# Output projection of a hybrid decoder layer: six tiles by plain blocks, ten by seven half-size products

## The chip, the cores and the metric

One Trainium2 chip, one core of it. The metric is the device time of one execution in microseconds; of several executions the median is given.

## The reference, cut to what matters

One layer over 2048 tokens of width 1024, all in float32. Two mixers work side by side on one input projection: an S5 state space mixer of width 256 and a Mamba-2 (SSD) mixer of width 768. The SSD mixer ends in an RMSNorm. Their outputs are joined, multiplied by `w_out` and added to the input:

```
y = y * gelu_gate                             # S5, 256 columns
ssd = rmsnorm(y_ssd * silu(z), norm_w)        # 768 columns
x = x + concatenate([y_s5, ssd]) @ w_out      # 1024 x 1024
```

After it come a cross-attention into 256 memory tokens and a gated MLP with a causal convolution, and a final norm.

## The kernel before, in words

Tiles are 128 tokens. A float32 operand is split into a high half and a low half (`halves`, lines 95 to 102: ScalarE copies to the rounded type, VectorE subtracts), and each product of two 128-wide blocks is three matmuls (`mm3`, lines 120 to 125): high by high, high by low, low by high. A matmul takes 128 x 128 of the left operand as weights and streams 512 columns of the right.

The mixers run first. For each 512 tokens `MixerIn.ssq` (line 503) gets the sums of squares of the SSD output and makes `rs`, the factor of the RMSNorm, one number a token, kept on chip; the SSD output itself is written to `yTd` in DRAM without it (the norm's weight is in). `yTd` is laid out transposed: channels on the partitions, eight blocks of 128 channels, blocks 0 and 1 from S5 and 2 to 7 from SSD. The S5 stage (`stage_s5`, line 771) runs beside the preparation of the attention's factors `G` and `VW`. It ends with four calls of `glu` (line 868), one for each 512 tokens, which write the S5 blocks of `yTd`. They lack a factor of 0.5.

Then `stage_b` (line 1094) does the output projection, the attention scores and the attention values. In the projection the weights are all 8 x 2 blocks of `w_out`, 128 x 512 each, split and held on chip in pools Q0 to Q3 (`W`). For each of 16 tiles of tokens, `yprep` (line 1113) loads the tile of `yTd` and of `x` two tiles ahead and splits the former. For each half of the columns there are two sums on PSUM: blocks 2 to 7 (SSD) and blocks 0 and 1 (S5). VectorE adds the first, multiplied by `rs`, to the tile of `x` (line 1215), then the second, multiplied by 0.5 (line 1216). The result goes to `x1d` by POOL's DMA queue (line 1217).

The scores and the values are done by pairs of tiles in another way. `products` (line 1008) takes 256 x 1024 by 1024 x 1024 as two by two blocks and does seven products of half size instead of eight (Strassen's method in Winograd's form), in the order 1, 6, 5, 3, 7, 4, 2. Each product is 4 x 3 matmuls of 512 columns. `lefts` (line 1154) makes the seven left factors of a pair with transposes by TensorE, four sums on VectorE and seven splits; `factors` (line 1135) makes the four right factors that are sums, from four blocks, and writes them to DRAM, and `right` (line 1146) loads a right factor and splits it. `factors("G", j)` is called at tiles 2, 4, 6 and 8 of the projection, and `right("G", m)` for three of the seven m in the last three tiles and for the others behind them. `factors("VW", p)` is called in the first four pairs of the scores, `right("VW", m)` in the last pair, each m right behind the product of that number, whose buffers it takes over.

Instructions stand in the program in the order in which Python emits them. A scheduler sets the order on each engine and queue: of what its model of time says is ready and has a buffer, what was emitted first goes first. So loads on the SP queue run ahead of their place when a buffer is free; a load that waits for a buffer holds what is behind it. The pools that matter: F (10 buffers of 128 x 512, raw loads and sums), A (16, split left operands), X (6 of 128 x 1024, tiles of x), Q (7 x 8, split right operands), and 8 buffers of PSUM, which `tr4` (transposes) and the products share.

Of the kernel before, what the change touches and what calls it, by code (L numbers as in the profile page):

```python
# [9 lines left out]
F32 = mybir.dt.float32  # L10
# [3 lines left out]
ALU = mybir.AluOpType  # L14
# [15 lines left out]
class Kit:  # L30


    def __init__(self, tc, cx):
# [12 lines left out]
        nc.vector.memset(self.m05, -0.5)  # L46
        self.gains = self.cp.tile([P, 32], F32, name="gains")
# [126 lines left out]
class MixerIn:  # L174
# [328 lines left out]
    def ssq(self, b, sqacc):  # L503
        k = self.k
        for _ in range(5):
            yield
        pq = k.ps()
        for c in range(4):
            k.TE.matmul(pq[:, c:c + 1], sqacc[:, c * 128:c * 128 + 128], self.one, start=True, stop=True)
        k.rstd(self.d["rs"][:, b * 4:b * 4 + 4], pq[:, 0:4], 0.25 / 768, 1e-6)  # L510
        yield
# [259 lines left out]
def stage_s5(k, a, d, T):  # L771
# [4 lines left out]
    with ExitStack() as cx:  # L776
# [91 lines left out]
        def glu(b, gs):  # L868
            for o in range(2):
# [4 lines left out]
                V.scalar_tensor_tensor(th, th, 1.0, gf[o, b], op0=ALU.add, op1=ALU.mult)  # L874
                G.dma_start(out=d["yT"][b * 4:b * 4 + 4, :, o, :].rearrange("c p n -> p c n"), in_=th.rearrange("p (c n) -> p c n", c=4))
# [218 lines left out]
def stage_b(k, cx, a, d, T, after):  # L1094
# [5 lines left out]
    Q = lambda i: (f"Q{i}", 8)  # L1100
    xl, xp, q4, mp, ap, *qs, fp = k.pools(cx, "b", ("L", 2, 1024), ("X", 6, 1024), Q(4), ("M", 4, 576), ("A", 16), Q(0), Q(1), Q(2), Q(3), Q(5), Q(6), ("F", 10))
    qs.insert(4, q4)
    tmp = lambda: mp()[:, 0:512]
    qp = ring(8, qs)

    def split(src, pl):
        hi, lo = pl(F32R), pl(F32R)
        k.halves(src, hi, lo)
        return hi, lo

    W, ys = {}, {}
# [23 lines left out]
    def factors(nm, j):  # L1135

        r = {(q, n): k.load(d[nm][q * 4 + j][:, n * 512:n * 512 + 512], fp()) for q in range(2) for n in range(2)}
# [5 lines left out]
        for i, t in enumerate((t1, t2, t3, t4)):  # L1143
            G.dma_start(out=d[nm + "t"][i, j], in_=t)

    def right(nm, m, lo=None):
        out = []
        for j in range(4):
            src = {1: d[nm][j][:, 0:512], 3: d[nm][4 + j][:, 512:1024], 2: d[nm][4 + j][:, 0:512],
                   5: d[nm + "t"][0, j], 6: d[nm + "t"][1, j], 7: d[nm + "t"][2, j], 4: d[nm + "t"][3, j]}[m]  # L1150
            out.append(split(k.load(src, fp()), qp))
        return out

    def lefts(x0, x1):
        a11, a21, a22, a12 = (fp() for _ in range(4))
        for o, x, hf in ((a11, x0, 0), (a21, x1, 0), (a22, x1, 1), (a12, x0, 1)):
            S.activation(o, k.tr4(x, hf), AF.Copy)
        yield split(a11, ap)
# [25 lines left out]

    early = (2, 3, 6, 7)
    with k.tc.issue_after(after.ins):
        for kt in early:
            W[kt] = [split(k.load(a["w_out"][kt][:, n * 512:n * 512 + 512], fp()), qp) for n in range(2)]
    first = [yprep(t, ((256, 512), (512, 1024), (0, 256))) for t in range(2)]
    for g in first * 2:  # L1190
        next(g)
    for kt in (4, 5, 0, 1):
        W[kt] = [split(k.load(a["w_out"][kt][:, n * 512:n * 512 + 512], fp()), qp) for n in range(2)]
    for g in first * 2:
        next(g)
    head = {(t, nh): proj(ys[t][0], nh, early, last=False) for t in range(2) for nh in range(2)}
    Rg = {}
    for t in range(NT):
        if t + 2 < NT:
            list(yprep(t + 2, ((0, 512), (512, 1024))))  # L1200
        act, x = ys.pop(t)
        if t + 2 == NT:
            gen, L = xprep(0), {}
        if t + 2 >= NT:
            for _ in range(2):
                L[ORDER[len(L)]] = next(gen)
# [385 lines left out]
```

## Time and profile before

| | |
|---|---|
| median of 3 runs | 2671.1 us (2668.69 to 2675.19) |
| the profiled execution | 2667.42 us, of which the span of the trace is 2665.7 |
| mean granted clock of TensorE | 0.994 |
| TensorE busy (matmuls) | 2603.0 us, 98% |
| VectorE, ScalarE busy | 2121.5 us (80%), 1358.0 us (51%) |
| POOL busy | 407.3 us (15%) |
| DMA | 480.94 MB, 180 GB/s over the span |

The engines are TensorE (PE, its weight loads PEld), VectorE (DVE), ScalarE (ACT) and GpSimd (POOL); SP issues most of the loads. An instruction's line is that of the helper that issued it, so a matmul of any stage is at lines 123 to 125, and its operands tell the stage: Q and A are the right and left operands of stage B. Busy time is a share of time and says nothing of how closely instructions of one engine follow one another; for that the starts in the timeline are read.

### The profile page before, as it was taken

Reading aid. Unit: us, or ns where it says so; the run is one execution under the profiler, and the core shown is the slowest. Engines: PE = TensorE matmul, PEld = TensorE weight load, DVE = VectorE, ACT = ScalarE, POOL = GpSimd, SP = SyncE. Lnnn points to the kernel's source line nnn. Section 1 sums busy time; section 2 is a strip of 40 time slices with the busy share of each in tenths; the row PEclk is TensorE's granted clock in tenths of the full one; section 3 lists DMA queues with packets and bytes.
Section 4 is the critical chain, followed back from the end, with each engine's and each line's share of the span. In section 5 each row is a group of like instructions: output and inputs, shape, how many; then the busy total and the mean of one; then the engine's idle time right before and its main releaser. Section 6 shows DMA issues by size and latency. Waiting matters only on the chain. (4 is left out here: it accounts for less than half of the span.)

```text
span 2665.7 us, 38967 instructions
## 1 busy us (share of the span) xinstructions
PE 2603.0 (98%) x12796; PEld 2150.3 (81%) x12796; DVE 2121.5 (80%) x4034; ACT 1358.0 (51%) x2817; POOL 407.3 (15%) x691
## 2 busy tenths in 40 slices
PE   8999999999999999999999999999999999999998
PEld 6768878788987888888888888888888887788876
DVE  8798898888876537778788878989787877678776
ACT  4655567764556116788554545445444434433333
POOL 1112212111022101202202332212111110000000
PEclk9999999999999999999999999999999999999999
DMA  5565554543586936546762444344222218887886
GB/s 188 173 186 175 182 192 164 164 139 126 177 303 235 336 126 213 182 168 231 261 202 83 128 146 133 103 123 153 80 87 80 87 64 280 278 283 249 262 263 209
DMA packets 244355, 480.94 MB, mean 180 GB/s; under 512 B 30584, under 2 KB 72824, under 8 KB 244152
## 3 DMA queue, kind: packets, MB, share of 16 engines
q1 hardware_dynamic: 182312, 341.38, 38.3%
q0 software_dynamic: 32976, 118.09, 13.8%
q10 hardware_dynamic: 28864, 18.98, 2.3%
q8 instruction: 101, 1.65, 0.3%
q14 instruction: 102, 0.84, 0.1%
HBM read 363.25 MB, written 114.49 MB: 179 GB/s over the span
## 5 line engine op out<-in xcount | busy, mean ns | idle before, releaser
L124 PE MATMUL ps<-H,W 128*128 128x512 f32 x952 | 370.6, 389 | 0.3 <-DVE H L99 0.3
L123 PE MATMUL ps<-H,W 128*128 128x512 f32 x952 | 370.8, 390 | 0.0
L125 PE MATMUL ps<-H,W 128*128 128x512 f32 x952 | 370.4, 389 | 0.0
L123 PE MATMUL ps<-h,w 128*128 128x512 f32 (+1 forms) x736 | 299.1, 406 | 3.1 <-DVE h L102 2.1
L124 PE MATMUL ps<-h,w 128*128 128x512 f32 (+1 forms) x736 | 286.6, 389 | 0.9 <-DVE h L102 0.9
L125 PE MATMUL ps<-h,w 128*128 128x512 f32 (+1 forms) x736 | 286.3, 389 | 0.7 <-DVE w L99 0.7
L123 PE MATMUL ps<-Q,A 128*128 128x512 f32 x704 | 275.8, 392 | 0.8 <-ACT A L98 0.8
L125 PE MATMUL ps<-Q,A 128*128 128x512 f32 x704 | 274.5, 390 | 0.2 <-DVE A L99 0.2
L124 PE MATMUL ps<-Q,A 128*128 128x512 f32 x704 | 273.9, 389 | 0.0
L98 ACT ACTIVATE W<-S 128x512 fp32r<-128x512 f32 x191 | 119.0, 630 | 292.8 <-DVE S L1346 146.1
L98 ACT ACTIVATE w<-r 128x512 fp32r<-128x512 f32 x224 | 139.4, 627 | 139.5 <-PE ps L124 108.7
L124 PEld LDWEIGHTS ps<-H,W 128*128 128x128 f32 x952 | 178.7, 188 | 38.0 <-DVE H L99 1.1
L125 PEld LDWEIGHTS ps<-H,W 128*128 128x128 f32 x952 | 178.7, 188 | 37.2
L123 PEld LDWEIGHTS ps<-H,W 128*128 128x128 f32 x952 | 178.7, 188 | 37.0 <-ACT H L98 0.3
L99 DVE TENSOR_TENSOR w<-r,w 128x512 fp32r<-128x512 f32 x224 | 153.5, 687 | 33.0 <-ACT w L98 31.4
L125 PEld LDWEIGHTS ps<-h,w 128*128 128x128 f32 x736 | 139.4, 189 | 30.6 <-DVE w L99 1.1
L123 PEld LDWEIGHTS ps<-h,w 128*128 128x128 f32 x736 | 139.6, 190 | 29.7 <-DVE h L102 2.3
L124 PEld LDWEIGHTS ps<-h,w 128*128 128x128 f32 x736 | 139.8, 190 | 27.6 <-DVE h L102 2.5
L125 PEld LDWEIGHTS ps<-Q,A 128*128 128x128 f32 x704 | 132.2, 188 | 29.1 <-DVE A L99 1.4
L123 PEld LDWEIGHTS ps<-Q,A 128*128 128x128 f32 x704 | 132.2, 188 | 27.8 <-ACT A L98 1.0
L124 PEld LDWEIGHTS ps<-Q,A 128*128 128x128 f32 x704 | 132.3, 188 | 26.6
L98 ACT ACTIVATE A<-F 128x512 fp32r<-128x512 f32 (+1 forms) x146 | 89.1, 631 | 126.4 <-PE ps L124 74.1
(474 smaller groups left out, 6187.4 us busy)
## 6 DMA issues: line engine op xcount, KB each, us to landing
A<-actd SPq DMA_DIRECT2D x192, 256.0 KB, 3.6
r<-in_w_in SPq DMA_DIRECT2D x176, 256.0 KB, 2.9
R<-in_w_up SPq DMA_DIRECT2D x176, 256.0 KB, 2.8
R<-in_w_down SPq DMA_DIRECT2D x132, 256.0 KB, 4.3
actd<-U POOLq DMA_DIRECT2D x88, 256.0 KB, 3.1
A<-actd SPq DMA_DIRECT2D x96, 192.0 KB, 3.6
R<-h3Cd SPq DMA_DIRECT2D x56, 256.0 KB, 3.2
L<-acsd POOLq DMA_DIRECT2D x32, 384.0 KB, 4.4
```

The lines of the kernel that those rows point to most:

```text
L98: self.S.activation(hi, src, AF.Copy)
L99: self.V.tensor_tensor(lo, src, hi.bitcast(F32), op=ALU.subtract)
L123: self.TE.matmul(out, lh, rh, start=first and i == 0, stop=False)
L124: self.TE.matmul(out, lh, rl, start=False, stop=False)
L125: self.TE.matmul(out, ll, rh, start=False, stop=last and i == n - 1)
```

## The change

The SSD norm's factor is taken out of the sum: the S5 blocks are divided by it, so that one sum over all eight blocks can be multiplied by `rs`. `ssq` makes `iv` = 0.5 / `rs` as well (a power on POOL) and writes it to DRAM; `glu` loads it, broadcast to all partitions, and multiplies with it.

The first three pairs of tiles (six tiles) are done by plain blocks as before, now with one sum per half and one scaled addition. Beside tiles 1 to 4, four blocks of `w_out` are loaded again for each j, and `tfour` makes the four sums from them; three of them are split on chip for right factors 6, 5 and 7, the fourth goes to `Otd` in DRAM and is loaded and split for right factor 4 behind the sixth tile, into the buffers of the plain weights that are no longer needed. Right factors 1, 2 and 3 are blocks of the plain weights already there. The other five pairs are done by `products`. Their left factors come from `yTd` without transposes (`ypair`). `factors("G")` moves to the first four of these pairs, and all seven `right("G", m)` to the last one. The pools of right operands are named by m and by half (`at`), at the same places of memory in sum.

```diff
         pq = k.ps()
         for c in range(4):
             k.TE.matmul(pq[:, c:c + 1], sqacc[:, c * 128:c * 128 + 128], self.one, start=True, stop=True)
+        iv = self.sp.tile([P, 4], F32, tag="iv", name="iv")
+        k.V.tensor_scalar(iv, pq[:, 0:4], 0.0625 / 768, 0.25e-6, op0=ALU.mult, op1=ALU.add)
         k.rstd(self.d["rs"][:, b * 4:b * 4 + 4], pq[:, 0:4], 0.25 / 768, 1e-6)
+        k.G.tensor_tensor(iv, iv, k.p05[:, 0:1].to_broadcast([P, 4]), op=ALU.pow)
+        k.G.dma_start(out=self.d["iv"][b].rearrange("(c p) -> p c", p=P), in_=iv)
         yield
...
         def glu(b, gs):
+            iv = k.t()
+            G.dma_start(out=iv, in_=d["iv"][b].partition_broadcast(P))
             for o in range(2):
...
                 V.scalar_tensor_tensor(th, th, 1.0, gf[o, b], op0=ALU.add, op1=ALU.mult)
+                V.tensor_tensor(th, th, iv, op=ALU.mult)
...
+    at = lambda m, j: qs[f"Q{m}{'ba'[j // 2]}"]
+    PLAIN = 3
...
+    kt_at = {(0, 0): 1, (0, 1): 4, (1, 0): 2, (1, 1): 3}
+
+    def wload(kt):
+        W[kt] = [split(k.load(a["w_out"][kt][:, n * 512:n * 512 + 512], fp()), at(kt_at[kt // 4, n], kt % 4)) for n in range(2)]
...
-        if t + 1 == NT:
-            for kts in ((2, 3), (6, 7)):
-                for nh in range(2):
-                    head[t, nh] = proj(act, nh, kts, head.get((t, nh)), last=False)
-        for nh in range(2):
-            s = slice(nh * 512, nh * 512 + 512)
-            p2 = proj(act, nh, (4, 5), head[t, nh]) if (t, nh) in head else proj(act, nh, range(2, 8))
-            p1 = proj(act, nh, [0, 1])
-            V.scalar_tensor_tensor(x[:, s], p2, d["rs"][:, t:t + 1], x[:, s], op0=ALU.mult, op1=ALU.add)
-            V.scalar_tensor_tensor(x[:, s], p1, 0.5, x[:, s], op0=ALU.mult, op1=ALU.add)
-        G.dma_start(out=d["x1"][t * 128:t * 128 + 128, :], in_=x)
-        if t in (2, 4, 6, 8):
-            factors("G", t // 2 - 1)
-        if t >= NT - 3:
-            Rg[ORDER[t - NT + 3]] = right("G", ORDER[t - NT + 3])
...
+    def ypair(p):
+        rows = []
+        for t in (2 * p, 2 * p + 1):
+            rows.append(k.load(d["yT"][t].rearrange("p a b -> p (a b)"), xp()))
+        (a11, a12), (a21, a22) = ((y[:, 0:512], y[:, 512:1024]) for y in rows)
+        return parts(a11, a21, a22, a12)
+    Rw, Rg, L = {5: [], 6: [], 7: []}, {}, {}
+    for t in range(2 * PLAIN):
+        j = t - 1
+        r = blocks(a["w_out"], j) if 0 <= j < 4 else None
+        if t + 2 < 2 * PLAIN:
+            list(yprep(t + 2, ((0, 512), (512, 1024))))
+        act, x = ys.pop(t)
+        if t == 2 * PLAIN - 3:
+            gen = ypair(PLAIN)
+        if t >= 2 * PLAIN - 2:
+            for _ in range(2):
+                L[ORDER[len(L)]] = next(gen)
+        for nh in range(2):
+            s = slice(nh * 512, nh * 512 + 512)
+            p = proj(act, nh, (4, 5, 0, 1), head[t, nh]) if (t, nh) in head else proj(act, nh, range(8))
+            V.scalar_tensor_tensor(x[:, s], p, d["rs"][:, t:t + 1], x[:, s], op0=ALU.mult, op1=ALU.add)
+        G.dma_start(out=d["x1"][t * 128:t * 128 + 128, :], in_=x)
+        if r:
+            t1, t2, t3, t4 = tfour(r)
+            G.dma_start(out=d["Ot"][j], in_=t4)
+            for m, v in ((6, t2), (5, t1), (7, t3)):
+                Rw[m].append(split(v, at(m, j)))
+    for m, q, n in ((1, 0, 0), (2, 1, 0), (3, 1, 1)):
+        Rw[m] = [W[q * 4 + j][n] for j in range(4)]
+    ahead = ypair(PLAIN + 1)
+    for m in ORDER[4:]:
+        L[m] = next(gen)
+    Rw[4] = [split(k.load(d["Ot"][j], fp()), at(4, j)) for j in range(4)]
+    for p in range(PLAIN, NP):
+        xs = []
+        for t in (2 * p, 2 * p + 1):
+            xs.append(xp())
+            nc.sync.dma_start(out=xs[-1], in_=a["x"][t * 128:t * 128 + 128, :])
+        gen, ahead = ahead, ypair(p + 2) if p + 2 < NP else xprep(p + 2 - NP)
+
+        def put(i, j, x, y, op):
+            c = tmp() if (i, j) == (1, 1) else x if i else y
+            V.tensor_tensor(c, x, y, op=op)
+            x = xs[i][:, j * 512:j * 512 + 512]
+            V.scalar_tensor_tensor(x, c, d["rs"][:, 2 * p + i:2 * p + i + 1], x, op0=ALU.mult, op1=ALU.add)
+
+        def after(m):
+            L[m] = next(gen)
+            if p + 1 == NP:
+                Rg[m] = right("G", m)
+            if m == 3 and p < PLAIN + 4:
+                factors("G", p - PLAIN)
+        products(k, terms(L, Rw), tmp, put, after)
+        for i in range(2):
+            t = 2 * p + i
+            G.dma_start(out=d["x1"][t * 128:t * 128 + 128, :], in_=xs[i])
...
-    ahead = xprep(1)
-    for m in ORDER[1:]:
-        if m not in Rg:
-            Rg[m] = right("G", m)
-        if m not in L:
-            L[m] = next(gen)
```

## Rows read from the trace of the kernel before

**Rows 1.** The page: busy time by engine; the granted clock in 40 slices.

```profile
PE 2603.0 (98%) x12796; PEld 2150.3 (81%) x12796; DVE 2121.5 (80%) x4034; ACT 1358.0 (51%) x2817; POOL 407.3 (15%) x691
...
PEclk9999999999999999999999999999999999999999
```

**Rows 2.** Busy time in stretches: us, then PE, PEld, DVE, ACT, POOL, clock, DMA share, GB/s.

```profile
836.00:848.00 12.00, 11.21 (x44) 8.41 (x45) 9.88 (x17) 11.61 (x24) 1.53 (x2) 0.86 0.59 193
...
870.00:890.00 20.00, 20.00 (x90) 16.57 (x89) 9.85 (x16) 3.71 (x6) 3.28 (x6) 1.00 1.00 363
...
970.00:990.00 20.00, 20.00 (x90) 16.57 (x89) 7.64 (x12) 1.90 (x3) 1.06 (x2) 1.00 0.13 52
...
1240.00:1260.00 20.00, 20.00 (x106) 17.05 (x105) 15.47 (x29) 14.78 (x39) 7.47 (x11) 1.00 0.71 239
```

**Rows 3.** The costliest groups: the first matmuls of stage B's products.

```profile
L123 PE MATMUL ps<-Q,A 128*128 128x512 f32 x704 | 275.8, 392 | 0.8 <-ACT A L98 0.8
```

**Rows 4.** Timeline of the projection, PE: start, duration; 39 matmuls between the two.

```profile
899.91 0.39 PE L123 MATMUL ps<-Q,A 128*128 128x512 f32 x1
...
908.75 0.39 PE L123 MATMUL ps<-Q,A 128*128 128x512 f32 x1
```

**Rows 5.** Timeline of the end of the scores, DVE.

```profile
1195.17 2.49 DVE L99 TENSOR_TENSOR Q<-F,Q 128x512 fp32r<-128x512 f32 x4
1197.58 0.69 DVE L1265 TENSOR_TENSOR X<-ps,M 128x512 f32<-128x512 f32 x1
```

**Rows 6.** Groups of DVE, 848 to 1031 us: busy, mean ns, idle before.

```profile
L1139 DVE TENSOR_TENSOR F<-F 128x512 f32<-128x512 f32 x4 | 2.8, 690 | 11.0 <-DMA F<-Gd 11.0
L1140 DVE TENSOR_TENSOR F<-F 128x512 f32<-128x512 f32 x4 | 2.8, 690 | 4.4 <-DMA F<-Gd 4.4
```

**Rows 7.** Timeline of the scores, PE: transposes of two successive pairs.

```profile
1154.40 1.91 PE L148 MATMUL ps<-ident,L 128*128 128x128 f32 x16
...
1175.22 1.91 PE L148 MATMUL ps<-ident,L 128*128 128x128 f32 x16
```

**Rows 8.** Waits of PE, 1000 to 1400 us: total, times, longest.

```profile
PE ps L123 <- ACT A L98: 0.8, 1, 0.8
PE ps L1068 <- ACT F L1157: 0.4, 1, 0.4
PE ps L124 <- DVE H L99: 0.3, 1, 0.3
```

**Rows 9.** Timeline of POOL: the sixth of sixteen writes of a finished tile.

```profile
926.36 0.54 POOL L1217 DMA_DIRECT2D x1d<-X  x1 [2.78 <-DVE X L1216]
```

**Rows 10.** Timeline of the SP queue: reads of G, first and fourth round.

```profile
866.24 2.37 SPq L111 DMA_DIRECT2D F<-Gd  x4
...
909.48 0.91 SPq L111 DMA_DIRECT2D F<-Gd  x2
...
913.18 2.56 SPq L111 DMA_DIRECT2D F<-Gd  x2
```

**Rows 11.** DMA issues: count, KB each, median us to landing.

```profile
L<-acsd POOLq DMA_DIRECT2D x32, 384.0 KB, 4.4
...
F<-in_w_out SPq DMA_DIRECT2D x16, 256.0 KB, 5.1
Gtd<-F POOLq DMA_DIRECT2D x16, 256.0 KB, 4.4
F<-Gtd SPq DMA_DIRECT2D x16, 256.0 KB, 4.5
```

**Rows 12.** Timeline of the end of the S5 stage and the first tiles, PE and DVE.

```profile
836.79 0.73 PE L123 MATMUL ps<-t 128*128 128x512 f32 x2 [1.94 <-ACT t L98]
...
853.97 4.29 DVE L99 TENSOR_TENSOR Q<-F,Q 128x512 fp32r<-128x512 f32 x7
858.47 0.69 DVE L99 TENSOR_TENSOR Q<-F,Q 128x512 fp32r<-128x512 f32 x1 [0.21 <-ACT Q L98]
...
864.96 0.75 DVE L1215 SCALAR_TENSOR_TENSOR X<-ps,rs,X 128x512 f32<-128x512 f32 x1
```

More of the change, by code (lines that the diff above doesn't have):

```diff
@@ L46, in __init__ @@
         nc.vector.memset(self.m05, -0.5)
+        self.p05 = self.cp.tile([P, 1], F32, name="p05")
+        nc.vector.memset(self.p05, 0.5)
         self.gains = self.cp.tile([P, 32], F32, name="gains")
@@ L1098, in stage_b @@
     NP = NT // 2
-    Q = lambda i: (f"Q{i}", 8)
-    xl, xp, q4, mp, ap, *qs, fp = k.pools(cx, "b", ("L", 2, 1024), ("X", 6, 1024), Q(4), ("M", 4, 576), ("A", 16), Q(0), Q(1), Q(2), Q(3), Q(5), Q(6), ("F", 10))
-    qs.insert(4, q4)
+    q5 = [("Q5b", 4), ("Q5a", 4)]
+    late = [(f"Q{m}b", 4) for m in (1, 4, 3, 2)]
+    first = [(f"Q{m}a", 4) for m in (1, 4, 3, 2)]
+    names = [n for n, _ in q5 + first + late] + [f"Q{m}{h}" for m in (6, 7) for h in "ba"]
+    xl, xp, q50, q51, mp, ap, *qs, fp = k.pools(cx, "b", ("L", 2, 1024), ("X", 6, 1024), *q5, ("M", 4, 576), ("A", 16), *first, *late, *((n, 4) for n in names[10:]), ("F", 10))
+    qs = dict(zip(names, [q50, q51] + qs))
     tmp = lambda: mp()[:, 0:512]
-    qp = ring(8, qs)
+    at = lambda m, j: qs[f"Q{m}{'ba'[j // 2]}"]
+    PLAIN = 3
     def split(src, pl):
@@ L1133, in proj, with blocks, tfour @@
         return p
-    def factors(nm, j):
-        r = {(q, n): k.load(d[nm][q * 4 + j][:, n * 512:n * 512 + 512], fp()) for q in range(2) for n in range(2)}
+    def blocks(src, j):
+        return {(q, n): k.load(src[q * 4 + j][:, n * 512:n * 512 + 512], fp()) for q in range(2) for n in range(2)}
+    def tfour(r):
         t1, t2, t3, t4 = fp(), fp(), r[0, 1], r[1, 0]
@@ L1142, in factors @@
         V.tensor_tensor(t4, t2, r[1, 0], op=ALU.subtract)
-        for i, t in enumerate((t1, t2, t3, t4)):
+        return t1, t2, t3, t4
+    def factors(nm, j):
+        for i, t in enumerate(tfour(blocks(d[nm], j))):
             G.dma_start(out=d[nm + "t"][i, j], in_=t)
@@ L1150, in right @@
                    5: d[nm + "t"][0, j], 6: d[nm + "t"][1, j], 7: d[nm + "t"][2, j], 4: d[nm + "t"][3, j]}[m]
-            out.append(split(k.load(src, fp()), qp))
+            out.append(split(k.load(src, fp()), at(m, j)))
         return out
@@ L1157, in lefts, with parts @@
             S.activation(o, k.tr4(x, hf), AF.Copy)
+        yield from parts(a11, a21, a22, a12)
+    def parts(a11, a21, a22, a12):
         yield split(a11, ap)
@@ L1227, in terms @@
         return f
+    early = (2, 3, 6, 7)
+    with k.tc.issue_after(after.ins):
+        for kt in early:
+            wload(kt)
+    begin = [yprep(t, ((256, 512), (512, 1024), (0, 256))) for t in range(2)]
+    for g in begin * 2:
+        next(g)
+    for kt in (4, 5, 0, 1):
+        wload(kt)
+    for g in begin * 2:
+        next(g)
+    head = {(t, nh): proj(ys[t][0], nh, early, last=False) for t in range(2) for nh in range(2)}
+    def ypair(p):
[4 more added lines that the diff above has]
+        return parts(a11, a21, a22, a12)
```

24 lines of the change are left out of this document (1 added, 23 removed).

## Prediction, made before the changed kernel was run

> **What bounds the kernel now.** I read the page first, then the stretch of the projection, then the two places outside it that resemble what the change puts there. The page: TensorE (PE) is busy 98% of the span at a granted clock of 9 or more tenths in every slice [rows 1]. In the projection it has no gap at all: 20.00 of 20 us at 870 and at 970 us, at full clock, while VectorE (DVE) works 9.85 and 7.64 us [rows 2]. So here a matmul taken off PE is time taken off the end, as long as nothing else becomes late. How much time: the duration of one matmul in the groups, 389 to 392 ns [rows 3], is a latency; matmuls overlap. The pace is the step between starts. From the start at 899.91 to that at 908.75 us there are 39 matmuls of 128x512: 8.84 / 39 = 0.2267 us each [rows 4]. The group of line 123 with 704 matmuls [rows 3] is the whole of stage B: 256 of the projection (16 tiles x 2 halves x 8 blocks), 224 of the scores and 224 of the values (8 pairs x 7 products x 4 each); lines 124 and 125 hold as many again.
>
> **What the products give.** Before: 256 x 3 = 768 matmuls. After: six plain tiles, 6 x 2 x 8 x 3 = 288, and five pairs, 5 x 7 x 4 x 3 = 420; 708 in all, 60 fewer. yT lies in memory with its contraction on the partitions, so the new left factors need no transposes; those of x1 stay as they are. 60 x 0.2267 = **13.6 us** less. The two projection sums of a half (blocks 2 to 7, blocks 0 and 1) become one, with the same matmuls. The Trainium skill states another price: its page "TensorE: Matmul & The Clock Gate", section "Back-to-back issue gap", gives some 131 ns for a 512-column matmul in a sustained stream. By it the 60 would be worth 7.9 us as an estimate, and the gain after the losses below under the 0.3% line. The trace's 0.2267 us is the same kind of stream in this kernel, so it decides, and no chance goes to the other.
>
> **VectorE and ScalarE in the five pairs.** A DVE instruction of 128x512 takes a step of 0.602 us where it is not waiting: four in 2.41 us, 1195.17 to 1197.58 [rows 5]. A pair needs 7 low halves and 4 sums for the left factors, 11 for the products (two sums on PSUM for U2 and U4, one for U3, and two instructions for each of four quadrants), and, in pairs 3 to 6, 4 for `factors("G")`: 26 x 0.602 = 15.7 us against 84 x 0.2267 = 19.0 us of PE. The values stage has this very load, and there PE is busy 20.00 of 20 us beside 15.47 of DVE [rows 2]. I cost it at nothing; the cover is the 3.3 us that DVE has left per pair. `factors("G")` comes with four reads on SP and four writes on POOL. Where it stood, DVE waited 11.0 and 4.4 us for those reads, in all four calls [rows 6]; 3.9 us a call would use up the cover, and the low halves of the next pair's left factors are queued behind. But the reads stood there beside the reload of weights and a DVE with nothing else to do; in the pairs they are issued at the fourth product, with three products more before the next pair, so I take no loss, and 0.6 us a pair as the other bound. In the plain tiles a reload of four `w_out` blocks adds 4 sums and 3 splits, 7 x 0.602 = 4.2 us, and two scaled additions instead of four take 1.2 away; per 10.9 us tile (48 x 0.2267) DVE then has some 11 instructions, 6.6 us. Nothing lost there either.
>
> **The last pair.** `right("G")` makes 28 low halves; they stood beside the last three plain tiles, and now stand in pair 7. DVE has 50 x 0.602 = 30.1 us there, PE 19.0 and 1.8 for 16 transposes (a scores pair with its transposes takes 1175.22 - 1154.40 = 20.82 us [rows 7]). It falls 9.3 us behind. The nearest row is the end of the scores, where the same code makes the 28 factors of VW beside the same left factors, 7 sums and the softmax: 46 such instructions and more. The waits of PE there come to 0.8 + 0.4 + 0.3 us [rows 8], for eight PSUM buffers and factors made ahead take up the rest. Bounds 0 and 9.3; I take 1.4, since the row is the same code.
>
> **The switch from plain to seven products.** PE needs the right factors for product 6 one product (2.7 us) after the switch, those of product 4, which go out to Ot and come back, five products (13.6 us) after. In the old trace the sixth tile leaves at 926.4 [rows 9], so PE switches at about 925. The reload is the twin of the old reads of G: four blocks, four subtractions. Four such rounds were issued, the first at 866.2 and the last at 909.5 us [rows 10], so 14.4 us apart on the mean, one every second tile in the program. The new ones stand one tile earlier and every tile. Even at the old rhythm the last lands at 909.5 + 3.7 (its second half was issued at 913.2) + 5.1 for `w_out` [rows 11] = 918.3, and with 7 instructions is split by 922.5; Ot is written (4.4) and read (4.5) [rows 11] and split (4 x 0.602) by 934, needed at 925 + 13.6 = 938.6. Cost nothing, with 5 us to spare. Queued on SP behind these loads are yT and x of the next tiles. The x of pair 3 waits on SP for the writes of tiles 4 and 5, but is first needed at the fourth product, 10.9 us after the switch.
>
> **The end of the S5 stage.** Eight DVE multiplications, 8 x 0.602 = 4.8 us, four broadcasts on POOL's queue (nearest: the broadcast of acs, 4.4 us to landing [rows 11]) and four small tiles. All four `glu` calls lie at 836 to 854 us. From 853.97 DVE makes seven low halves of `w_out` in 4.29 us without a gap, and the last at 858.47 [rows 12]; the scaled additions of `glu` stand before them. The first projection sum is read at 864.96 [rows 12]. So 4.8 us more on DVE meets some 4 to 5 us of cover: a loss of 0 to 1 us. If a broadcast is late, DVE waits with all those low halves behind it, and PE after them. PE already waits 1.94 us at 836.79 [rows 12], and the clock of that stretch is 0.86 [rows 2], so 28% of 12 us at the lower of its two levels, which costs another 1.7. Moving tiles in that pool can save this or double it: bounds -3 and +4; I take +0.7, near the plain count. The square roots for `iv` (a power on POOL and one small write in each of four blocks) lie beside work that PE does not wait for.
>
> **Sum.** -13.6 + 1.4 + 0.7 = -11.5 us. The profiled execution took 2667.4 us (span 2665.7), 3.7 under the median of 2671.1; applied to the median, **2659.6 us**, 0.43% less. About 0.3% (8 us) is what a measurement of this kernel can tell from no change.
>
> **Rivals.**
> *DVE is late in the last pair for its whole arithmetic.* 9.3 us come back: -13.6 + 9.3 + 0.7 = -3.6, 2667.5. For it: 30.1 against 20.8. Against it: the 1.5 us of the scores' end [rows 8].
> *DMA, not PE, sets the pace of the first tiles.* The share of the DMA engines is 1.00 at 870 to 890 us with 363 GB/s [rows 2]; were matmuls merely spread by their data, taking some away gains nothing, and the reload only replaces reads of G: 2671. Against it: matmuls come as densely where the share is 0.13, with 90 in 20 us at both places [rows 2]. The Trainium skill warns of the busy share of matmuls, in "Perfetto Trace Analysis", section "Identifying the Most-Contended Engine": weight loads are to be looked at. The rows agree that weights load for 16.57 of 20 us, so the share alone proves little; the equal counts are what I rest on.
> *Right factors late at the switch (slower).* If a round of four reloads is spaced by more than (927.7 - 9.3 - 866.2) / 3 = 17.4 us, PE stands still at product 6; the 9.3 are landing and splitting. Spaced by 21 it eats the gain. At 24, because SP holds `w_out` loads behind an x or a yT load that waits for a buffer, PE loses 3 x 6.6 = 19.8 and some 2 more at the lower clock: -11.5 + 21.8 = +10.3, 2681. For it: four rounds now stand in four tiles, on the queue that carries everything. Against: 14.4 us between rounds in the old trace, with writes of Gt beside them that are gone.
> That the matmuls aren't fewer can't be: the loops are unrolled and their counts fixed.
>
> **Chances.** The forecast 0.62; an S5 end that shifts in our favour, near 2656, 0.05; DVE late 0.14; DMA pace 0.06; the switch a few us late, near 2667, 0.04; the switch late enough to be slower 0.09. So faster 0.67, within 0.3% 0.24, slower 0.09. The low end is the full 13.6 with 3 us from the S5 end, 2654.5; the high end takes in the DVE rival and the spread of the runs, 2669. Left out are the slower case and most of the DMA one, some 0.15.
>
> **What would show it.** Right: 684 matmuls in each of the three groups of Q and A; steps of 0.2267 us; pairs of projection 19.1 us apart with PE full; the scores starting some 12 us earlier; DVE full and PE waits under 2 us at the last pair; rounds of `w_out` reads under 17 us apart. Wrong: waits of PE on low halves or on PSUM at the switch or before the scores, a drop of the granted clock there, or a longer gap before the first projection matmul with DVE waiting for `iv`.

## The result, and the profile after

The changed kernel takes 2684.8 us (median of 5; 2681.7 to 2695.5) against 2671.1 for the kernel before beside it: ratio 1.0062, interval 1.0047 to 1.0078, 0.6% slower. Forecast were 2659.6 and a range of 2654.5 to 2669.0; the sign is wrong. The executions of one kernel spread by up to 14 us (one of e5, at 6689 us, is left out), so below a stage is read from one profile and a whole from ratios.

The matmuls went as counted. In the page after, PE has 60 instructions fewer than in [rows 1], and its idle share has grown.

```profile
PE 2598.9 (97%) x12736; PEld 2142.8 (80%) x12736; DVE 2167.0 (81%) x4117; ACT 1379.5 (51%) x2853; POOL 421.4 (16%) x707
...
PEclk9999999999999999999999999999999999999999
```

Three stretches lost this again, and more. Busy time by stretches after (columns as in [rows 2]): the entry of S5, the first tiles, a pair of the projection, its last pair, the first pair of the scores.

```profile
732.00:736.00 4.00, 4.00 (x36) 4.00 (x35) 1.25 (x3) 0.63 (x1) 1.51 (x3) 1.00 1.28 147
736.00:740.00 4.00, 2.09 (x18) 1.89 (x16) 0.00 (x0) 0.48 (x1) 0.00 (x0) 1.00 0.78 134
740.00:744.00 4.00, 2.28 (x9) 1.99 (x10) 3.77 (x7) 2.77 (x7) 0.00 (x0) 0.70 0.98 362
...
870.00:890.00 20.00, 16.61 (x72) 13.42 (x73) 14.75 (x25) 5.15 (x9) 3.55 (x5) 1.00 0.89 311
...
970.00:990.00 20.00, 20.00 (x90) 16.58 (x89) 16.30 (x30) 4.75 (x8) 4.84 (x8) 1.00 0.64 215
...
1008.05:1028.85 20.80, 20.80 (x101) 17.48 (x100) 17.46 (x32) 10.38 (x23) 2.18 (x4) 1.00 0.70 244
1028.85:1058.87 30.02, 23.33 (x101) 18.39 (x100) 27.90 (x50) 21.72 (x42) 2.59 (x4) 0.94 0.84 288
```

*Entry of S5.* Between 732 and 740 us the DMA engines are busy at 1.28 and 0.78 (a share over 1 means packets that overlap) and move 147 and 134 GB/s. From 734 us DVE has no work and ACT 0.48 us of it, then PE has none, and the granted clock falls to 0.70 of full, a mean over its two levels, 1.2 and 2.4 GHz. Before, the same 732 to 736 us read so:

```profile
732.00:736.00 4.00, 4.00 (x33) 3.73 (x32) 1.95 (x4) 2.55 (x6) 0.00 (x0) 1.00 1.03 399
```

What POOL issued just ahead is the last of four writes of `iv`, 512 numbers of 4 bytes each; this is the view of `ivd` after, with the writes and the four later copies.

```profile
L516 POOL DMA_DIRECT2D ivd<-iv x4: 799/808/811, 266.9 to 727.9; - x4
L876 POOL DMA_DIRECT2D t<-ivd x4: 538/554/554, 843.4 to 863.8; - x4
...
  DVE t L883: 3.8, 2
```

The view of `iv` has the four writes alone; 2 KB take 8 to 12 us to land:

```profile
DMA to landing us min/median/max: 8.3/9.6/11.7
```

*End of S5.* DVE waits 3.59 us for a broadcast of `iv`, behind it stand the low halves that PE needs (timelines of DVE and PE after). That answers to [rows 12], where DVE had no such gap. From the first projection matmul to the end of the sixth tile it takes 71.8 us, 67.7 before.

```profile
869.83 2.50 DVE L883 TENSOR_TENSOR t<-t 128x512 f32<-128x512 f32 x4 [3.59 <-DMA t<-ivd]
```

```profile
872.98 0.50 PE L127 MATMUL ps<-Q2a,A 128*128 128x512 f32 x1 [3.15 <-DVE A L101]
```

*Behind the last pair.* In the last pair itself (the stretch from 1008.05 us) PE is full. The first pair of the scores takes 30.0 us, 20.8 before. These are the first matmuls of the first two pairs of the scores, in the timeline after:

```profile
1028.85 0.39 PE L125 MATMUL ps<-Q1b,A 128*128 128x512 f32 x1
...
1058.87 0.39 PE L125 MATMUL ps<-Q1b,A 128*128 128x512 f32 x1
```

DVE is busy 27.90 of these 30.02 us, with low halves of G's right factors and the last evacuations of the projection (line 1271, in `put`), and PE waits for the latter. The waits of PE from 1000 to 1400 us, against the 1.5 us of [rows 8]:

```profile
PE ps L125 <- DVE M L1271: 6.5, 3, 2.7
PE ps L125 <- DVE su L1297: 1.4, 1, 1.4
PE ps L125 <- ACT H L100: 0.9, 1, 0.9
```

Between them, from 880 to 1020 us, PE is full, the pairs and the switch included.

### The profile page after: what moved, and what is told of

Read it like the earlier page. It is cut to its first block, busy times and chain, and to the rows that moved or that the text cites. A ratio compares the mean times of both kernels' runs of the same rounds, so it can differ in the third digit from the quotient of the medians.

```text
span 2680.0 us, 39005 instructions
## 1 busy us (share of the span) xinstructions
PE 2598.9 (97%) x12736; PEld 2142.8 (80%) x12736; DVE 2167.0 (81%) x4117; ACT 1379.5 (51%) x2853; POOL 421.4 (16%) x707
## 3 DMA queue, kind: packets, MB, share of 16 engines
q1 hardware_dynamic: 183752, 346.62, 39.9%
## 5 line engine op out<-in xcount | busy, mean ns | idle before, releaser
L315 DVE SCALAR_TENSOR_TENSOR t<-t,cw 128x512 f32<-128x512 f32 x168 | 129.0, 768 | 13.9 <-ACT t L313 12.9
L101 DVE TENSOR_TENSOR W<-S,W 128x512 fp32r<-128x512 f32 x191 | 130.5, 686 | 7.9 <-ACT W L100 6.2
L100 ACT ACTIVATE W<-R 128x512 fp32r<-128x512 f32 x124 | 76.6, 628 | 112.9 <-PE ps L126 102.3
L1464 DVE SCALAR_TENSOR_TENSOR U<-G,C,U 128x512 f32<-128x512 f32 x176 | 122.9, 748 | 13.5 <-POOL G L1457 8.7
L127 PE MATMUL ps<-W,B 128*128 128x512 f32 x308 | 121.8, 396 | 6.9 <-DVE B L101 6.1
L1513 DVE TENSOR_TENSOR A<-A 128x512 f32<-128x512 f32 (+1 forms) x120 | 77.0, 645 | 60.7 <-DMA A<-actd 59.5
```

Of the source, the lines that this page charges most:

```text
L100: self.S.activation(hi, src, AF.Copy)
L101: self.V.tensor_tensor(lo, src, hi.bitcast(F32), op=ALU.subtract)
L127: self.TE.matmul(out, ll, rh, start=False, stop=last and i == n - 1)
L315: k.V.scalar_tensor_tensor(xc, gb[:, q:q + 512], cw[:, j, q:q + 1], xc, op0=ALU.mult, op1=ALU.add)
L1464: V.scalar_tensor_tensor(q4(c), g[:, :, q:q + 128], cw[:, i, q:q + 1], q4(c), op0=ALU.mult, op1=ALU.add)
L1513: V.tensor_tensor(raws[0], raws[0], raws[1], op=op(l[2]))
```

## The experiments

All comparisons are with the kernel before, run beside each. "Rows" below is the kernel of e5. The columns are: the stretch from the first load of `in_wqT` to the first of `in_wo` (SP queue); the start of the first projection matmul; from it to the first matmul of the seventh tile (not given where the order of the tiles is another); the first two pairs of the scores; the time from the first projection matmul to the last transposes of the values; ratio and interval.

| kernel | wqT to wo | projection starts | six tiles | two scores pairs | to the values' end | ratio |
|---|---|---|---|---|---|---|
| before | 24.3 | 848.6 | 67.7 | 41.6 | 484.3 | 1 |
| after | 29.4 | 860.1 | 71.8 | 50.8 | 484.4 | 1.0062 (1.0047 to 1.0078) |
| e1 no iv | 23.7 | 849.1 | 67.7 | 52.6 | 484.1 | 0.9992 (0.9981 to 1.0003) |
| e2 iv alone | 30.2 | 865.1 | 72.4 | 41.6 | 489.3 | 1.0038 (1.0024 to 1.0051) |
| e3 iv on chip | 23.5 | 876.2 | 65.3 | 51.1 | 478.3 | 1.0069 (1.0051 to 1.0087) |
| e4 priority | 30.2 | 862.9 | 72.2 | 52.5 | 486.1 | 1.0064 (1.0041 to 1.0087) |
| e5 rows | 21.2 | 849.7 | 68.6 | 50.7 | 481.4 | 1.0000 (0.9989 to 1.0011) |
| e8 early copies | 31.7 | 861.5 | 69.7 | 49.8 | 481.7 | 1.0062 (1.0047 to 1.0077) |
| e6 rows, no low halves | 21.6 | 848.8 | 68.9 | 50.2 | 481.7 | 0.9999 (0.9990 to 1.0009) |
| e7 rows, GpSimd | 21.6 | 851.3 | 69.2 | 57.5 | 488.7 | 1.0041 (1.0026 to 1.0056) |
| e9 rows, 7 reads | 21.7 | 848.7 | 68.7 | 47.2 | 478.2 | 0.9988 (0.9979 to 0.9998) |
| e10 rows, neither | 21.8 | 854.5 | 70.2 | 45.8 | 477.2 | 0.9976 (0.9965 to 0.9987) |
| e13 rows, no factors | 21.8 | 853.4 | 72.3 | 41.6 | 475.8 | 0.9976 (0.9965 to 0.9988) |
| e15 no iv, no factors | 24.6 | 852.9 | 67.7 | 41.6 | 470.4 | 0.9965 (0.9953 to 0.9978) |
| e11 plain pair last | 21.9 | 853.5 | - | 41.6 | 489.9 | 1.0025 (1.0014 to 1.0036) |
| e12 and early sums | 22.1 | 852.6 | - | 41.6 | 482.8 | 0.9994 (0.9983 to 1.0006) |
| e14 and lighter | 22.3 | 855.0 | - | 41.6 | 477.3 | 0.9996 (0.9986 to 1.0005) |
| e16 and early scale | 21.9 | 851.5 | - | 41.6 | 481.3 | 0.9992 (0.9981 to 1.0004) |

### The inverse root: e1 to e3, e5, e8

**e1**, the changed kernel without `iv`.

```diff
-        k.G.dma_start(out=self.d["iv"][b].rearrange("(c p) -> p c", p=P), in_=iv)
...
-                V.tensor_tensor(th, th, iv, op=ALU.mult)
```

> The changed kernel without iv: neither the square root and the write in ssq nor the broadcast and the multiplications in glu (the S5 blocks of yT lack their factor). Theory 1, from the two traces: what iv brings (the writes of 4 bytes an element at the entry of the S5 stage, POOL's queue in the mixer, the broadcasts at its end) costs 10 to 14 us, so this runs at 2668 to 2675 us, and the S5 stage's first matmul of line 834 is back near 755 us. Rival: the losses come from the order in which the scheduler puts things since the program differs, and iv itself is cheap: 2680 to 2688 us. If only the last pair had cost anything, it would also stay above 2680.

2669.8 us, ratio 0.9992. The loss goes, but none of the 13.6 us shows as a gain.

**e2**, the kernel before with `iv` and one factor for both sums.

```diff
-            V.scalar_tensor_tensor(x[:, s], p1, 0.5, x[:, s], op0=ALU.mult, op1=ALU.add)
+            V.scalar_tensor_tensor(x[:, s], p1, d["rs"][:, t:t + 1], x[:, s], op0=ALU.mult, op1=ALU.add)
```

> The kernel before with iv alone: ssq, glu and the factor rs in place of 0.5 on the second sum; the projection stays sixteen plain tiles. Theory 1: slower than before by 10 to 14 us, 2681 to 2685, nearly all of it ahead of the first projection matmul; the projection itself as long as before. Rival: iv lies beside other work, 2669 to 2674 us, and the loss of the changed kernel is in the pairs.

Ratio 1.0038, 10 us more, without any of the products. So `iv` by itself costs most of it.

**e3**, `iv` kept on chip and spread by four diagonal matrices and four matmuls by ones in each `glu`.

```diff
+            for c in range(4):
+                cs = slice(c * 128, c * 128 + 128)
+                V.tensor_scalar(dg[:, cs], k.ident, d["iv"][:, b * 4 + c:b * 4 + c + 1], None, op0=ALU.mult)
+                TE.matmul(iv[:, cs], ones, dg[:, cs], start=True, stop=True)
```

> The changed kernel with iv kept on chip: one small tile for all tokens, and in glu four diagonal tiles and four matmuls by ones that spread it over the partitions, with no DMA. Theory 1 (the DMAs of iv are what costs): 2668 to 2676 us, some 1 us above the run without iv. Rival (the multiplications on VectorE and the power on POOL are what costs, or the scheduler's order): 2680 us and more.

A miss: ratio 1.0069. The entry of S5 is back at 23.5 us, but PE, in order, now waits in `glu` for the diagonals behind a busy DVE (waits of PE, 720 to 900 us):

```profile
PE ps L880 <- DVE t L879: 17.1, 4, 6.4
```

**e5**, the same factor in another form: collected on chip in a 128 x 16 tile, turned once, written as 16 rows of 512 bytes, the copies read at the start of S5.

```diff
+        TE.transpose(pv[0:T // 128, 0:P], d["iv"][:, :], k.ident)
+        S.activation(ivr, pv[0:T // 128, 0:P], AF.Copy)
+        G.dma_start(out=d["ivd"], in_=ivr)
```

> Edit: the changed kernel, with the inverse roots kept in a small tile on chip; at the start of S5 four PE instructions' worth of work turn the 128x16 tile round once, one DMA writes it as 16 rows of 512 bytes, and the four copies for all partitions are read right after, into tiles of their own. The 16 multiplications in the gated units stay. Theory 1 (the 4-byte writes and the late copies cost the time, the multiplications do not): 2671, between 2667 and 2676; from the first in_wqT load to the first in_wo load about 24 us, no wait of DVE on the copies in the gated units. Rival (the scheduler's other order and the added VectorE work cost it, however the factor travels): 2680 or more.

2669.7 us, ratio 1.0000: the loss of the change is gone with all its arithmetic still there (the multiplications are 8, not 16). The entry of S5 takes 21.2 us.

**e8**, the 4-byte writes kept, only the copies early.

```diff
-            iv = k.t()
-            G.dma_start(out=iv, in_=d["iv"][b].partition_broadcast(P))
...
+        for b in range(T // 512):
+            G.dma_start(out=ivs[b], in_=d["iv"][b].partition_broadcast(P))
         inp(0)
```

> Edit: the changed kernel with its four writes of 512 x 4 bytes as they are, but the four copies for all partitions read early in S5 into tiles of their own, instead of one ahead of each gated unit. Theory 1 with two shares (the writes cost some 5 us at the entry of S5, the late copies some 4 us at its end): 2681, between 2678 and 2684, that is 7 to 12 us more than the kernel with rows; the stretch from the first in_wqT load to the first in_wo load stays near 29 us. Rival (the writes cost nothing that PE waits for, all of it is the late copies): within 3 us of the kernel with rows.

2684.5 us, just above my range: the late copies cost nothing in the sum, and more than the 5 us of my share hangs on the writes, since e5 differs from this kernel in their form alone. S5 in this kernel stops in full for 4 us while the last of them lands (same columns as above):

```profile
736.00:740.00 4.00, 3.59 (x31) 3.39 (x29) 0.69 (x1) 0.63 (x1) 0.00 (x0) 1.00 1.18 204
740.00:744.00 4.00, 0.00 (x0) 0.00 (x0) 0.00 (x0) 0.00 (x0) 0.00 (x0) 0.93 0.75 195
```

Early copies take 2.1 us off the six tiles and put 2.3 on the entry, so the wait for a broadcast seen in the kernel after is not what the change lost by. In the table every kernel with 4-byte writes has 29 to 32 us in the first column, every other 21 to 25.

### The last pair: e4, e6, e7, e9, e10, e13, e15

**e4**, the changed kernel, evacuations of the last projection pair put ahead of the splits.

```diff
+        with k.tc.high_priority(pri) if pri else nullcontext():
...
-        products(k, terms(L, Rw), tmp, put, after)
+        products(k, terms(L, Rw), tmp, put, after, 200 if p + 1 == NP else 0)
```

> The changed kernel with a higher priority for what reads the products of the last projection pair (the copy and the sums on PSUM and the scaled additions), so that they go ahead of the splits of G's right factors on VectorE. Theory 2: PE's 6.5 us of waits there and some 2 us at the lower clock are waits for PSUM behind those splits; 5 to 8.6 us come back, 2676 to 2680 us. Rival: VectorE's load of 30 us in that pair is what counts, whatever its order; PE then waits for G's right factors in the first pair of the scores instead, and the time stays at 2682 to 2687.

A miss: ratio 1.0064. The waits on line 1271 went; PE then waited in the first pair of the scores for the right factors and at the second for a left one, and the two take 52.5 us against 50.8. Order moved the wait, not the sum.

**e6**, rows without the 28 low halves.

```diff
+                hi = at(m, j)(F32R)
+                S.activation(hi, src, AF.Copy)
+                out.append((hi, hi))
```

> Edit: the kernel of the run before (rows) with one more: the 28 right factors of the scores that are made in the last projection pair have no low halves (the products use the high half twice, so the matmul count stays; the low part of G is left out of the computation). Theory 2 (VectorE's load in the last pair costs some 8 us): 8 us less than the kernel with rows, between 5 and 10, and PE busy over 19.5 of every 20 us from 1000 to 1060. Rival (the reads of the factors, or ScalarE, would take VectorE's place): at most 3 us less.

A miss: ratio 0.9999. I had held VectorE alone for the cause. With e5 and e6 side by side (stretches, columns as above) DVE falls from 18.91 to 6.00 us, and PE still does 69 matmuls where 98 fit; the DMA engines are at 0.93 and 0.88. The two scores pairs take 50.2 us, 50.7 in e5.

```profile
1020.00:1040.00 20.00, 14.38 (x54) 10.53 (x55) 18.91 (x33) 15.67 (x31) 1.11 (x2) 0.91 0.93 321
```

```profile
1020.00:1040.00 20.00, 15.96 (x69) 12.31 (x67) 6.00 (x13) 14.53 (x29) 1.45 (x3) 1.00 0.88 338
1040.00:1060.00 20.00, 18.79 (x79) 15.77 (x80) 16.68 (x32) 15.30 (x36) 3.51 (x7) 0.83 0.53 172
```

PE's wait is now one of 4.4 us on ScalarE's copy of a left factor of the second scores pair, whose rows of x1 were issued on SP behind the last reads of G (waits of PE, 1000 to 1060 us).

```profile
PE ps L125 <- ACT A L100: 4.4, 1, 4.4
```

**e7**, rows with half of the low halves on GpSimd.

```diff
+                G.tensor_tensor(lo, src, hi.bitcast(F32), op=ALU.subtract)
```

> Edit: the kernel with rows, and 14 of the 28 low halves of the scores' right factors in the last projection pair are subtracted by GpSimd instead of VectorE. Theory 2: VectorE is relieved of 14 x 0.60 = 8.4 us of its some 60 in 1000 to 1066, so the 8 us of PE waits shrink by at least half: 4 to 8 us less than the kernel with rows, below the kernel before. Rival (GpSimd is slower at it than 1.5 us each, or holds VectorE up): the same as the kernel with rows or slower, and PE waits on the low halves that GpSimd makes.

The rival held: ratio 1.0041. GpSimd takes some 1.3 us for one and stops VectorE meanwhile (last section).

**e9**, rows with 7 reads instead of 28, and **e10**, with 7 reads and no low halves (the edits of e9 and e6 together).

```diff
+            if j == 0:
+                one = k.load(src, fp())
+            out.append(split(one, at(m, j)))
```

> Edit: the kernel with rows; of the scores' 28 right-factor blocks made in the last projection pair only 7 are read (each of the seven factors takes its first block four times; the other three blocks of each are left out of the computation), all 28 are still split in two halves. Theory 3 (in the last pair VectorE and the reads are both full, and either alone keeps PE waiting some 10 us): the same as the kernel with rows, within 3 us, with PE still waiting on VectorE. Rival (the reads alone set the pace, VectorE is late only beside them): 6 to 10 us less.

> Edit: the kernel with rows, with 7 reads instead of 28 and no low halves for the scores' right factors (both left out of the computation; the matmul count stays). Theory 3: 8 to 12 us less than the kernel with rows, about 2660, and PE busy over 19.5 of every 20 us from 1000 to 1060. Rival (something else, such as ScalarE's copies or the second pair of x1 rows, holds PE there): within 3 us of the kernel with rows.

Ratios 0.9988 and 0.9976. Low halves away gives 0.0%, reads away 0.1%, both away 0.24%; with intervals of 0.1% either way that doesn't show whether both give more than the sum of the two. And 0.24% is 6.4 us and not the 8 to 12 expected. The two scores pairs say more: of the 9.1 us that they lose in e5, the low halves give back 0.5, the reads 3.6, both 4.9. Without the reads DVE is the full one (26.30 of 26.30 us in the first scores pair of e9), and without both ScalarE (19.11 of 20 us in e10, where PE waits for it). These are the stretches of e9 and e10, columns as above, and PE's wait in e10 from 1020 to 1050 us:

```profile
1014.50:1040.80 26.30, 22.61 (x102) 18.55 (x100) 26.30 (x48) 18.03 (x38) 2.69 (x4) 0.94 0.42 141
```

```profile
1020.00:1040.00 20.00, 17.80 (x84) 14.51 (x83) 11.13 (x22) 19.11 (x41) 2.22 (x4) 0.95 0.56 195
```

```profile
PE ps L125 <- ACT M L1033: 2.2, 1, 2.2
```

So three limits lie close together, and relieving one leaves the next. A rival was not tried: the factors start late. In e5 DVE is busy 11.34 us of the last projection pair's 20.80 and 28.52 of the next 29.90, and ScalarE, in order, stands 6.0 us for the rows of x1 before its first copy of a factor (stretches and ScalarE's timeline of e5).

```profile
994.40:1015.20 20.80, 20.80 (x101) 17.47 (x100) 11.34 (x22) 9.60 (x21) 2.18 (x4) 1.00 0.50 177
1015.20:1045.10 29.90, 23.70 (x101) 18.16 (x100) 28.52 (x51) 22.57 (x43) 2.60 (x4) 0.94 0.90 299
```

```profile
1003.92 0.63 ACT L1059 ACTIVATE F<-L 128x512 f32<-128x512 f32 x1 [5.99 <-DMA L<-x1d]
```

**e13**, rows with no right factors made in the last pair at all.

```diff
-                Rg[m] = right("G", m)
+                Rg[m] = Rw[m]
```

> Edit: the kernel with rows, with the last projection pair making none of the scores' right factors (no reads, no copies, no low halves: the scores use the projection's factors in their place, so G is left out of the computation; the matmul count stays). Theory 4 (all of the missing gain of 13.6 lies in making the right factors inside the one last pair; ScalarE's 28 copies are the part that the kernel with neither reads nor low halves still paid): 10 to 14 us less than the kernel with rows, about 2658, and under 1 us of PE waits from 1000 to 1060. Rival (part of the gain is lost in another place, such as the end of S5 or the switch): the same as with neither reads nor low halves, about 2664.

In the profile the pairs are healed, 98 matmuls in 20 us throughout and 41.6 us for the two scores pairs. The whole came to 2661.7 against 2668.3, less than expected and the rival's number. To the values' end 8.5 us of the 13.6 are there; 4.6 are lost at the end of S5, at 860 us, where the six tiles take 72.3 us against 67.7 (stretches of e13).

```profile
860.00:880.00 20.00, 17.58 (x70) 13.72 (x69) 12.77 (x22) 4.97 (x9) 2.43 (x4) 0.91 0.95 340
1020.00:1040.00 20.00, 20.00 (x98) 16.82 (x97) 14.80 (x28) 9.30 (x20) 2.21 (x4) 1.00 0.47 159
```

**e15**, neither right factors nor `iv` (the edits of e13 and e1).

> Edit: the changed kernel without the inverse roots (as in the first experiment) and with the last projection pair making none of the scores' right factors (S5's factor and G are left out of the computation). Account: of the 13.6 us that 60 matmuls are worth, the last pair took some 10 and the multiplications at the end of S5 some 3. With both gone nothing is left to take: 2656 against about 2670 before, between 2653 and 2660, and PE full from 840 to 1100 as in the kernel before. Rival (there is a third loss in the projection, or the matmuls are worth less than their pitch): 2662 or more.

Both places are full (stretches of e15):

```profile
860.00:880.00 20.00, 20.00 (x90) 16.54 (x89) 11.49 (x20) 5.98 (x12) 2.67 (x5) 1.00 0.95 330
1020.00:1040.00 20.00, 20.00 (x98) 16.78 (x98) 11.24 (x22) 7.96 (x18) 2.21 (x4) 1.00 0.49 159
```

From the first projection matmul to the values' end it takes 470.4 us, 13.9 less than before, where 60 matmuls are worth 13.6. The whole is 2662.3 against 2672.2, ratio 0.9965: 9.4 us, not 14, and the rival's number, though the stretch leaves no room for its reasons. In its profile, the slowest of its six executions, S5 ended 4 us later and the stages after the values took some 10 longer than in the profile before. These stages have the same code in both, and one profile each doesn't tell spread from effect (in e5 to e7, e9, e10 and e13, which have one code ahead of it, the projection starts at 848.7 to 854.5 us); that part stays open.

### Spreading the burst: e11, e12, e14, e16

**e11**, rows with two plain pairs at the start and one at the end, so that the scores' factors are made in two pairs.

```diff
-    PLAIN = 3
+    PLAIN, PAIRS = 2, 5
...
+                if m in (6, 5, 7):
+                    Rg[m] = right("G", m)
...
+        if nh == 0:
+            Rg[1] = right("G", 1)
+            ahead = xprep(1)
+            Rg[2] = right("G", 2)
```

> Edit: the kernel with rows, with the three plain pairs placed two at the start and one at the end of the projection (the fourth block of w_out is read again for the last one); the seven right factors of the scores are made in the last product pair (5, 6, 7), the last plain pair (1, 2) and after it (3, 4). Same matmul count. Theory 3 (the burst of right factors in one product pair is the price): the waits of 10 us shrink to under 3: 2662, between 2656 and 2667, faster than both kernels. Rival (two plain pairs are too short for making the right factors on chip, or the reads of w_out collide): PE waits at the switch or in the last plain pair, 2669 or more.

A miss: ratio 1.0025. PE waited 12.5 us in the last product pair, where ScalarE, and behind it DVE, stood for a load of yT (timelines of ScalarE, then PE).

```profile
1003.40 0.63 ACT L100 ACTIVATE A<-F 128x512 fp32r<-128x512 f32 x1 [9.89 <-DMA F<-yTd]
```

```profile
1010.14 1.12 PE L150 MATMUL ps<-ident,L 128*128 128x128 f32 x4 [12.53 <-DVE M L1277]
```

That load was queued on SP behind reads of Gt, and these behind the write of Gt and the x1 rows: SP's own waits.

```profile
SPq L1272 <- DMA x1d<-X: 8.6, 2, 7.3
SPq L113 <- DMA Gtd<-F: 5.6, 1, 5.6
```

**e12**, the sums of G a pair earlier.

```diff
-            if m == 3 and p < PLAIN + 4:
-                factors("G", p - PLAIN)
+            if (p - PLAIN, m) in early_g:
+                factors("G", early_g[p - PLAIN, m])
```

> Edit: the kernel with a plain pair at the end, with the sums of G's blocks made in the first three product pairs (one, two, one) instead of one in each of four, so that they are written and landed a whole pair before the last product pair reads them. Theory (the 12.5 us that PE waited in the kernel with the plain pair at the end were VectorE held in order behind a block of Gtd that was written too late; without that the spread of the right factors pays): 2664, between 2659 and 2668. Rival (VectorE and the reads fill the last product pair as they filled the last pair before, so the wait only changes its name): 2670 or more.

Ratio 0.9994, the rival's number: SP's wait for Gt is gone and PE's 12.5 us are 5.3, the rest stays. **e14** took one factor out of that pair, **e16** then moved the multiplications in S5 ahead of the gated unit.

```diff
-                if m in (6, 5, 7):
+                if m in (6, 5):
...
-                V.tensor_tensor(th, th, ivs[b], op=ALU.mult)
...
+                    V.tensor_tensor(gf[i, b], gf[i, b], ivs[b], op=ALU.mult)
```

> Edit: the kernel with a plain pair at the end and early sums, with one factor less in the last product pair: the fourth block of w_out goes into factor 7's place, factor 4 is made in the first plain tile, and factor 7 after the projection. So the last product pair makes 8 blocks of factors and 4 of w_out instead of 12 and 4. Theory 4: the 10 us that PE lost in 980 to 1020 shrink by about half: 2666, between 2661 and 2670. Rival (the wait follows the load into the plain pair or the first scores pair): 2671 as with early sums.

> Edit: the kernel with the lighter last product pair, in which the eight multiplications by the inverse roots are moved from behind each gated unit onto its other factor, ahead of it, right after that factor is split. Everything is computed. Account: the last multiplication leaves the chain that ends S5, VectorE's sum stays: 1 to 3 us less than the kernel with the lighter last product pair, 2666. Rival (VectorE is full there, so the order does not matter): the same, 2668 to 2669.

0.9996 and 0.9992, neither apart from 1, from e12 nor from the other: by the ratios both rivals held, though PE's 5.3 us are 0.4 in the profile of e14. No kernel that computes everything came out faster than the kernel before. e5 repairs the change; the forecast gain was not had.

## Why the prediction was wrong

**The 13.6 us stand.** 12796 - 12736 = 60 matmuls; the ten tiles that are now five pairs take 97.0 us after and 110.6 before, and e15 shows 13.9 us less between the same two events. The pitch of [rows 4] was the right price, and the 7.9 us by the Trainium skill's page "TensorE: Matmul & The Clock Gate", section "Back-to-back issue gap", was rightly set aside.

**Where the loss lies.** In the two profiles the changed kernel starts its projection 11.5 us later than before, takes as long to the values' end (484.4 against 484.3 us) and 2.7 us longer behind it. So two terms of the sum ate the gain, and what stands ahead of the projection made the loss. The prediction had named this sign of being wrong, a longer gap before the first projection matmul, and had no price for it.

**The step that failed first: "The square roots for `iv` (a power on POOL and one small write in each of four blocks) lie beside work that PE does not wait for."** True of the arithmetic, wrong of the write, which I never priced. It is 2 KB and looked like nothing, but in pieces of 4 bytes. Its price is after against e5, which keeps the multiplications: 1.0062 against 1.0000, some 16 us (15.1 by the medians; 14.8 from e8, where the copies are early too). About 8 us of it are at the entry of S5 (29.4 against 21.2). By the same two profiles 3.5 lie ahead of it (first load of `in_wqT` at 726.1 and 722.6 us), 3.2 in the six tiles and 2.5 behind the values, with 1.3 won back between; how much of these is spread, one profile each doesn't tell. It was the only part of the change that is outside the stretch I studied, and I gave it half a sentence and no row.

**"Bounds 0 and 9.3; I take 1.4, since the row is the same code."** The rival I gave 0.14 came true, one pair later than it was put: the last pair keeps its 20.8 us, and the first pair of the scores loses 9.2 us after and 9.1 in e5. The end of the scores [rows 8] is the same program text for `right`, but not the same load: there `put` is one DVE instruction a quadrant, here two, and the reads of x and the writes and reads of x1 share the queues with the factors (which of these counts was not tried). There DVE was busy 34.3 us of the 41.7 that the last scores pair and the first values pair took; here it has 45.4, more than fit into two pairs. My own count, 30.1 us of DVE against 20.8 of PE, was the better evidence. I set it aside for a resemblance. But that its 9.3 is so close to 9.2 is luck in part: e5 has 39.9 us of DVE and loses as much, with the low halves away (e6) 8.6 are still lost, and with both away 4.2 (e10).

**"I take +0.7, near the plain count" for the end of S5** was too small. The six tiles, 67.7 us before and in e1 and e15 without the multiplications, take 71.8 after, 4.1 more, just above my upper bound of 4. With early copies they take 0.9 more (e5) to 4.6 (e13).

**The five pairs at nothing**: right. They take 19.0 us each, and PE is full beside 16.30 us of DVE in 20, where the values had 15.47 for the same load [rows 2]. The 0.6 us a pair of the other bound did not come.

**The switch at nothing**: right. The last read of `Otd` was issued at 922.7, the sixth tile left at 938.4, and PE had no wait between 880 and 1020. The rival that would have been slower played no part.

**The sum** of the stretch with measured terms: for the kernel after -13.6 + 9.2 + 4.1 = -0.3, and its profile shows 0.1. The rest of the result, some 14 us, lies outside the stretch, 11.5 of it ahead, and goes with the form of the writes: e5 has 1.1 ahead and 0.2 behind. For e5 -13.6 + 9.1 + 0.9 = -3.6, where its profile shows -2.9; as a whole it measured 0.0% with an interval of 3 us either way.

## What to carry to other kernels

Price every added DMA by its pieces, not by its bytes, and look at what else is on the wire when it lands; a vector that lies across the partitions is turned on chip and written in rows. When work is moved into one pair, add it up for each engine and for the queue that feeds it, believe the sum over a place that looks alike, and look for the wait in the pair behind it as well. Where limits stand close together, relieving one shows little: take them away together in one run before giving any up.

## What was not expected of the hardware

**A write in 4-byte pieces holds up large loads beside it.** Around it the engines' busy share was 1.25 to 1.32 while they moved 198 and 96 GB/s (2 us stretches after), against 1.03 with 399 GB/s before.

```profile
732.00:734.00 2.00, 2.00 (x19) 2.00 (x18) 1.25 (x3) 0.63 (x1) 1.51 (x3) 1.00 1.25 198
734.00:736.00 2.00, 2.00 (x19) 2.00 (x18) 0.00 (x0) 0.00 (x0) 0.00 (x0) 1.00 1.32 96
```

In the trace's records of single packets the write itself is 16 packets of 128 bytes and 0.04 us each, from 731.3 us on. But from 732.3 to 740.3 us there are 26 packets of 4 KB that take over 1.5 us, up to 3.8, where the median is 0.16. Such packets (up to 4 KB, over 1.5 us, from 715 to 750 us) number 29, 24 and 19 in e2, e4 and e8, which write in the same way, none before and in e5, and at most 6 in any kernel without these writes. So the records show the price on the neighbours and don't show how the write takes it.

The Trainium skill's page "DMA: Bandwidth & Descriptors", section "Specifications", says that below 512 bytes a transfer falls short of line rate, by a read-modify-write. The rows agree that short pieces are dear (8.3 us and more to landing, 2.6 for the 512-byte rows of e5); no row shows a read-modify-write.

**A GpSimd instruction can stop VectorE for its whole length.** In e7 three GpSimd subtractions follow each other from 1032.30 to 1036.05 us, and a VectorE subtraction of the same shape, 0.68 us otherwise, lasts from 1032.22 to 1036.60. One with an operand in PSUM takes 0.68 at 1042.99 us, beside a GpSimd subtraction of 1.29 (timelines of POOL and DVE).

```profile
1032.30 1.30 POOL L1182 TENSOR_TENSOR Q3b<-F,Q3b 128x512 fp32r<-128x512 f32 x1
1033.56 1.28 POOL L1182 TENSOR_TENSOR Q3a<-F,Q3a 128x512 fp32r<-128x512 f32 x1
1034.80 1.25 POOL L1182 TENSOR_TENSOR Q7b<-F,Q7b 128x512 fp32r<-128x512 f32 x1
...
1042.93 1.29 POOL L1182 TENSOR_TENSOR Q2b<-F,Q2b 128x512 fp32r<-128x512 f32 x1 [0.42 <-ACT Q2b L1181]
```

```profile
1032.22 4.38 DVE L101 TENSOR_TENSOR Q3a<-F,Q3a 128x512 fp32r<-128x512 f32 x1
...
1042.99 0.68 DVE L1039 TENSOR_TENSOR M<-ps,M 128x512 f32<-128x512 f32 x1
```

The Trainium skill's page "SBUF — State Buffer", section "SBUF: two separate sides", calls the pair of ports that the two engines share an exclusive lock, held for a whole instruction, against which a VectorE operation with two operands in SBUF blocks. The rows agree that it blocks; by their times the VectorE subtraction had begun 0.08 us ahead of the first GpSimd one, and it still lasted through all three.
